# Part of the first shift by matrix products at step 1, and products of ones at the start, in a two-layer encoder kernel on one core

## The chip, the cores and the metric

The kernel runs on one core of a Trainium2 chip. The metric is the device time of one execution in microseconds (us); lower is better. The engines are TensorE (PE; its weight loads are shown as PEld), VectorE (DVE), ScalarE (ACT), GpSimd (POOL) and SyncE (SP), which issues the DMAs. Each engine runs its own list of instructions, and semaphores order the lists against each other.

## The reference, cut to what matters

Two layers of a streaming encoder, 256 tokens by 1024 channels. The part that matters here is the head of layer 0: a vector c is turned into six vectors by a matrix product, and the first two of them scale and shift the normalised input before the input projection.

```python
c_act = jax.nn.silu(c)
mod = jnp.dot(c_act, w_mod[layer]) + b_mod[layer]
sh1, sc1, g1, sh2, sc2, g2 = jnp.split(mod[:, None, :], 6, axis=-1)
u = rms_norm(x, norm1_g[layer]) * (1.0 + sc1) + sh1
x = x + g1 * token_mixers(u, ...)      # projection by w_in, three mixers, merge
u = rms_norm(x, norm2_g[layer]) * (1.0 + sc2) + sh2
x = x + g2 * grouped_moe(u, ...)       # 16 experts, 2 per token
```

Everything is float32; `w_mod` is 1024 x 6144, so `sh1` and `sc1` each need 4 MB of weights before the last channel of `u` is known.

## The kernel before, in words

The program is one list of calls per engine; the order in the code is the order on each engine (the schedule is manual). Weights come as blocks of up to 1 MB in the order of `plan`, through seven buffers `raw0` to `raw6`; SP issues the next block when a buffer has been given back, so a block lands some way ahead of its use.

Layer 0 begins with `prologue`: loads, constants, the row `crow` (c spread to 128 partitions by PE, L355, and put through SiLU by ACT, L357), then the sums of squares of x (ACT squares, L480, and PE products with a single column, L489). `rstd` (L524, L526) and `spread` (L534, L536) make of them the factor that every channel is multiplied by.

The first shift and scale are computed in two ways. `mod_rows` (L453) does it by DVE: 256 rows of the transposed weights against `crow`, two dot products over 1024 numbers, then the bias (L463) and for the scale one more instruction (L466). `mod_matmul` (L426) does it by PE: two blocks of 512 columns, eight products, then a copy by ACT (`mod_copy`, L433), four transposes by PE, a sum by DVE and the bias (`mod_finish`, L440, L442, L463). In the kernel before, all of the first shift and scale comes from `mod_rows`; later vectors of both layers use `mod_matmul`.

The start of the projection is cut into four steps (in `mixers`, layer 0). Step s takes two of the eight groups of 128 channels. It calls `mod_rows(0, s)` for the shift and `mod_rows(0, 4 + s)` for the scale, then one part of `modulate`: `uv` by DVE (L566), its high part `uh` by ACT (L567), its low part `ul` by DVE (L570). Then for each of three column blocks, gB0, gB1 and bi, `split_to` cuts half a weight block into a high part `h` by ACT (a CAST, L282) and a low part by DVE (a subtraction, L283), and PE makes the products (gB0 and gB1: 24 each, L615, L617, L618; bi: 12, L596 to L598). Nothing is split ahead in these steps. After step 1 `rotary` makes cosines and sines (L413 to L416). After step 3 the blocks' results are copied out by ACT (L924), and the next blocks (bq and on) follow, with a `mod_matmul` after bi.

`heat(n)` (L1180) issues n products of the identity by itself, whose result is not used; the kernel before calls it in the routing part of each layer and at the end of layer 0.

Of the kernel before, what the change touches and what calls it, by code (L numbers as in the profile page):

```python
# [10 lines left out]
F32 = mybir.dt.float32  # L11
# [97 lines left out]
WARM_IN = 1  # L109
HEAT_END = 4  # L110
HEAT_AFTER = 8


INNER = 'FVTS'
# [54 lines left out]
class Kernel:  # L169
# [30 lines left out]
    def t(self, pool, shape, dt, tag, bufs=1):  # L200
        return pool.tile(shape, dt, tag=tag, name=self.nm(tag), bufs=bufs)
# [101 lines left out]
    def prologue(self):  # L303
        nc, g, a = self.nc, self.g, self.a
        t = self.t
        self.sm = t(g, [128, SM_W], F32, "sm")
        nc.sync.dma_start(self.sm, a["smalls"])
        self.S = {k: self.sm[:, o:e] for k, (o, e) in SM.items()}
        self.cact_row()
        self.posi = t(g, [128, 2], I32, "posi")  # L310
        nc.sync.dma_start(self.posi, a["positions"])
        self.xT = t(g, [128, KT, T], F32, "xT")
        nc.sync.dma_start(self.xT, a["x"])
        self.pump()
        self.junk = t(g, [128, 1], F32, "junk")
        self.eps = t(g, [128, 1], F32, "eps")
        nc.vector.memset(self.eps, EPS)
        self.table(AF.Silu)
        self.ident = t(g, [128, 128], F32, "ident")
        make_identity(nc, self.ident)  # L320
        self.fold = t(g, [128, 16], F32, "fold")
        nc.vector.tensor_reduce(self.fold, self.ident.rearrange("p (q r) -> p r q", q=4)[:, 0:16], axis=AX.X, op=ALU.add)
        self.ones = t(g, [128, 128], F32, "ones")
        nc.vector.memset(self.ones, 1.0)
        self.ones_bf = t(g, [128, 128], BF16, "onesbf")
        nc.vector.memset(self.ones_bf, 1.0)
        self.tri = t(g, [128, 128], BF16, "tri")
        nc.vector.memset(self.tri, 1.0)
        nc.gpsimd.affine_select(self.tri, self.tri, pattern=[[1, 128]], compare_op=ALU.is_gt,
                                fill=0.0, base=0, channel_multiplier=-1)  # L330
        self.slot = t(g, [128, 128], F32, "slot")
        nc.gpsimd.iota(self.slot, pattern=[[1, 128]], base=-1024, channel_multiplier=0,
                       allow_small_or_imprecise_dtypes=True)
        self.up16 = t(g, [128, 16], F32, "up16")
        nc.gpsimd.iota(self.up16, pattern=[[1, 16]], base=0, channel_multiplier=0,
                       allow_small_or_imprecise_dtypes=True)
        self.down16 = t(g, [128, 16], F32, "down16")
        nc.gpsimd.iota(self.down16, pattern=[[-1, 16]], base=15, channel_multiplier=0,
                       allow_small_or_imprecise_dtypes=True)
        self.part = t(g, [128, 1], F32, "part")  # L340
        nc.gpsimd.iota(self.part, pattern=[[0, 1]], base=0, channel_multiplier=1, allow_small_or_imprecise_dtypes=True)
        self.mod = [t(g, [128, 6, 8], F32, f"mod{l}") for l in range(L)]
        self.scale = [[t(g, [128, 8], F32, f"sc{l}{j}") for j in range(2)] for l in range(L)]
# [89 lines left out]
        self.nc.scalar.copy(sb, acc)  # L433
        return sb

    def mod_finish(self, l, c, sb):
        nc = self.nc
        tp = self.psum("t")
        for b in range(4):
            nc.tensor.transpose(tp[:, 128 * b:128 * b + 128], sb[:, 128 * b:128 * b + 128], self.ident)  # L440
        j, k0 = divmod(4 * c, 8)
        nc.vector.tensor_reduce(self.mod[l][:, j, k0:k0 + 4],  # L442
                                tp.rearrange("p (b q r) -> p b q r", b=4, q=4)[:, :, :, 0], axis=AX.X, op=ALU.add)
        self.mod_bias(l, j, k0, 4)
# [438 lines left out]
    def mixers(self, l, parts, angles):  # L883
        nc, a = self.nc, self.a
# [3 lines left out]
        t = self.t  # L888
# [139 lines left out]
        if l == 0:  # L1028

            tags = iter(("mm", "mm", "mm", "y", "y", "y"))  # L1030
            for s in range(4):
                if s:
                    self.mod_rows(0, s)
                    self.mod_rows(0, 4 + s)
                next(parts)
                if s == 3:
                    self.ahead = AHEAD
                for i, c in enumerate(ORDER[:N_SPLIT]):
                    if s == 0:
                        open_chunk(c, tags, fine=True)  # L1040
                    next(gens[c])
                    if s == 3:
                        step_done(N_SPLIT + i, c, 1)
                if s == 1:
                    self.rotary(*angles)
            order = order[2 * N_SPLIT:]
        else:
            self.ahead = 0
            for s in range(4):
                next(parts)  # L1050
                if s == 3:
                    self.ahead = AHEAD
                for i, c in enumerate(ORDER[:N_EDGE]):
                    if s == 0:
                        open_chunk(c, iter(("mm", "mm") if i == 0 else ("mm", "y") if i == 1 else ("y", "y")), fine=True)
                    next(gens[c])
                    if s == 3:
                        step_done(N_EDGE + i, c, 1)
            order = order[2 * N_EDGE:]
# [113 lines left out]
        for c in "ckptmu":  # L1173
            assert next(acts[c], None) is None, c

    def heat(self, n):

        ps = self.hot if self.hot is not None else self.psum("mm")
        for _ in range(n):
            self.nc.tensor.matmul(ps[:, :128], self.ident, self.ident, start=True, stop=True)  # L1180

    def choose(self, l, aff, sel):

# [440 lines left out]
    def plan(self):  # L1624
# [27 lines left out]
        for l in range(L):  # L1652
            order = list(enumerate(half_order(l)))
            first = len(self.stream)
            if l == 0:
                for s in range(4):
                    rows(0, s).halved = 2
                    rows(0, 4 + s).halved = 2
                    for i, c in enumerate(ORDER[:N_SPLIT]):
                        n = COLS[c][1]  # L1660
                        key = ("in", l, c, s // 2)
                        if s % 2 == 0:
                            u = Unit(key, block("w_in", l, c, s // 2, n), n)
                            u.halved = 1
                            self.stream.append(u)
                        else:
                            u = Unit(("rest", *key), None)
                            u.rest = next(x for x in self.stream if x.key == key)
                            self.stream.append(u)
                            u = u.rest  # L1670
                        self.preps.append((u, s % 2))
                        if s == 3:
                            fill(0, N_SPLIT + i)
                order = order[2 * N_SPLIT:]
            together = []
            for s, (c, h) in order:
# [45 lines left out]
    def build(self):  # L1722
# [3 lines left out]
        for l in range(L):  # L1726
            with tc.tile_pool(name=f"w{l}", bufs=1) as self.w:
                if l == 0:
                    self.prologue()
                    self.fill_columns()  # L1730
                    self.fill_row()
                    angles = self.angles()
                    self.lam = self.lambdas()
                    next(self.lam)
                    acc = self.psum("y")
                    for k in range(4):
                        self.sum_squares(acc, k)
                    self.mod_rows(0, 0)
                    for k in range(4, KT):
                        self.sum_squares(acc, k)  # L1740
                    self.table(AF.Sqrt)
                    self.mod_rows(0, 4, (0,))
                    self.mod_rows(0, 4, (1,))
                    rstd = self.spread(self.rstd(acc), "t")
                rt = self.mixers(l, self.modulate(rstd, self.scale[l][0], self.mod[l][:, 0]), angles)
            with tc.tile_pool(name=f"e{l}", bufs=1) as self.e:
                self.slots += self.parts
                self.once += ONCES
                self.ye, self.ye_turn = None, 0
                self.parts = []  # L1750
                self.pump()
                self.where = {}
                self.route(l, rt)
                self.experts(l)
                self.parts = [x for x in self.slots if x[0] == "h"] + self.parts
                self.slots = [x for x in self.slots if x[0] == "r"]
            self.e = None
            rst = self.rstd(self.acc)
            if l == 0:
                self.heat(HEAT_END)  # L1760
            rstd = self.spread(rst, "y")
            if l == 0:
                self.heat(HEAT_AFTER)
# [64 lines left out]
```

## Time and profile before

| | us |
|---|---|
| median of 3 runs | 1067.27 (1066.63 to 1067.83) |
| profiled execution | 1067.82 |
| its span, first to last instruction | 1066.0 |
| PE busy | 1018.6 (96%) |
| DVE busy | 598.0 (56%) |
| ACT busy | 388.8 (36%) |
| DMA queue of loads, share of 16 engines | 79.8% |

A row of the time line gives the start, the time covered, the engine, the line, the operation, output<-input, and xN for N instructions merged; brackets give the idle time before it and what ended that. A row of the table of stretches gives the busy time of each engine in a stretch with its number of instructions, then TensorE's granted clock (1.00 is the higher of its two levels, 0.50 the lower, and between them a mean of both), the busy share of the DMA engines, and GB/s. A float32 product shows as two MATMUL rows.

### The profile page before, as it was taken

How to read it: one execution, taken by the hardware profiler on the slowest of the kernel's cores; microseconds unless marked ns; L12 is line 12 of the kernel's file. 1: busy time of each engine (PE TensorE's matmuls, PEld its weight loads, DVE VectorE, ACT ScalarE, POOL GpSimd, SP SyncE). 2: the span in 40 equal slices, each digit the busy share in tenths (PEclk: the TensorE clock that was granted, in tenths of full speed). 3: DMA queues.
4: the chain of work that ended last, by engine and by line, in shares of the span. 5: the costliest groups of instructions: out<-in, count | busy, mean ns of one | idle time of the engine just before them, and what ended most of it. 6: DMA issues, size and time to landing. Idle time of an engine off the chain costs nothing. (4 is left out here: it accounts for less than half of the span.)

```text
span 1066.0 us, 18867 instructions
## 1 busy us (share of the span) xinstructions
PE 1018.6 (96%) x7550; PEld 703.6 (66%) x7550; DVE 598.0 (56%) x1414; ACT 388.8 (36%) x736; POOL 1.5 (0%) x11
## 2 busy tenths in 40 slices
PE   7899999999999999799999999999998999979996
PEld 5789778799974343343489887789997534324344
DVE  6968898678842232222255799986885313222224
ACT  4445566654531111010245456675453201001022
POOL 0000000000000000000000000000000000000000
PEclk9999999999999999999989999999999999999998
DMA  9986768787967999999946465567784799999981
GB/s 345 366 353 236 269 263 336 297 335 277 353 245 306 395 420 421 420 420 421 403 176 242 194 237 198 198 224 279 307 339 163 304 397 420 420 419 420 422 351 40
DMA packets 53845, 336.56 MB, mean 316 GB/s; under 512 B 5617, under 2 KB 11889, under 8 KB 15474
## 3 DMA queue, kind: packets, MB, share of 16 engines
q1 hardware_dynamic: 53746, 335.25, 79.8%
q8 instruction: 61, 1.00, 0.4%
q14 instruction: 38, 0.31, 0.1%
HBM read 334.18 MB, written 1.05 MB: 314 GB/s over the span
## 5 line engine op out<-in xcount | busy, mean ns | idle before, releaser
L283 DVE TENSOR_TENSOR h<-raw,h 128x1024 fp32r<-128x1024 f32 (+1 forms) x132 | 154.7, 1213 | 32.0 <-ACT h L282 31.9
L1455 PE MATMUL mm<-raw,gb 128*32 128x512 f32 (+1 forms) x640 | 160.9, 596 | 1.6 <-DMA raw<-in_exp_w_dram 1.6
L615 PE MATMUL mm<-uh,h 128*128 128x256 f32 x480 | 138.9, 289 | 5.8 <-ACT h L282 5.8
L618 PE MATMUL mm<-uh,h 128*128 128x256 f32 x480 | 137.3, 286 | 2.7 <-DVE h L283 2.7
L282 ACT CAST h<-raw 128x1024 fp32r<-128x1024 f32 (+1 forms) x132 | 131.0, 1041 | 20.2 <-PE mm L618 9.8
L617 PE MATMUL mm<-ul,h 128*128 128x256 f32 x480 | 136.6, 285 | 0.0
L1535 DVE TENSOR_TENSOR x<-y,x 128x512 fp32r<-128x512 f32 (+1 forms) x34 | 22.5, 660 | 158.5 <-ACT x L1534 158.5
L1455 PE MATMUL mm<-h,gb 128*32 128x512 f32 (+1 forms) x376 | 101.4, 595 | 0.0
L615 PEld LDWEIGHTS mm<-uh,h 128*128 128x128 f32 x480 | 92.1, 192 | 11.8 <-ACT h L282 7.5
L1421 DVE SCALAR_TENSOR_TENSOR xT<-y,mod,xT 128x256 f32<-128x256 f32 x128 | 53.2, 477 | 73.7 <-PE y L1546 73.7
L1455 PE MATMUL mm<-x,gb 128*32 128x512 f32 (+1 forms) x456 | 94.5, 595 | 0.0
L618 PEld LDWEIGHTS mm<-uh,h 128*128 128x128 f32 x480 | 91.9, 192 | 3.7 <-DVE h L283 3.6
L617 PEld LDWEIGHTS mm<-ul,h 128*128 128x128 f32 x480 | 92.1, 192 | 0.0
L1455 PE MATMUL y<-raw,gt 128*32 128x512 f32 (+2 forms) x424 | 89.4, 570 | 1.4 <-ACT gt L1429 1.4
L1455 PEld LDWEIGHTS mm<-raw,gb 128*32 128x32 f32 (+1 forms) x640 | 41.1, 116 | 56.1 <-issue 49.9
L596 PE MATMUL mm<-h,uh 128*128 128x512 f32 (+1 forms) x176 | 70.7, 402 | 0.0
L597 PE MATMUL mm<-h,uh 128*128 128x512 f32 (+1 forms) x176 | 69.1, 393 | 0.0
L598 PE MATMUL mm<-h,ul 128*128 128x512 f32 (+1 forms) x176 | 69.1, 393 | 0.0
L1455 PE MATMUL y<-x,gt 128*32 128x512 f32 (+2 forms) x232 | 64.7, 580 | 0.7 <-ACT gt L1429 0.7
L453 DVE SCALAR_TENSOR_TENSOR raw<-raw,crow 128x1024 f32<-128x1024 f32 x52 | 62.0, 1219 | 1.0 <-ACT uv L480 1.0
L1365 ACT ACTIVATE gb<-y,mod,sc 128x256 f32<-128x256 f32 (+1 forms) x40 | 20.9, 521 | 107.5 <-DVE gb L1367 107.5
L1429 ACT COPY gt<-t 128x512 f32<-128x512 f32 x16 | 9.4, 585 | 128.1 <-PE t L1428 128.1
(317 smaller groups left out, 2008.2 us busy)
## 6 DMA issues: line engine op xcount, KB each, us to landing
raw<-in_exp_w_dram SPq DMA_DIRECT2D x77, 1024.0 KB, 15.5
x<-in_exp_w_dram SPq DMA_DIRECT2D x48, 1024.0 KB, 15.4
raw<-in_w_in_dram SPq DMA_DIRECT2D x43, 1024.0 KB, 5.1
h<-in_exp_w_dram SPq DMA_DIRECT2D x39, 1024.0 KB, 18.2
raw<-in_w_mod_dram SPq DMA_DIRECT2D x19, 1024.0 KB, 6.0
raw<-in_w_modt_dram SPq DMA_DIRECT2D x18, 1024.0 KB, 4.9
uh<-in_exp_w_dram SPq DMA_DIRECT2D x12, 1024.0 KB, 15.8
ul<-in_exp_w_dram SPq DMA_DIRECT2D x10, 1024.0 KB, 19.7
```

Of the source, the lines that this page charges most:

```text
L282: nc.scalar.copy(hi[:, :, :u.n], src)
L283: nc.vector.tensor_sub(lo[:, :, :u.n], src, hi[:, :, :u.n].bitcast(F32))
L453: nc.vector.scalar_tensor_tensor(v[:, b], v[:, b], 1.0, self.crow, op0=ALU.mult, op1=ALU.mult, accum_out=self.mod[l][:, j, k0 + b:k0 + b + 1])
L596: nc.tensor.matmul(o, uh, hi[:, k, :u.n], start=(kk == 0), stop=False)
L597: nc.tensor.matmul(o, uh, lo[:, k, :u.n], start=False, stop=False)
L598: nc.tensor.matmul(o, ul, hi[:, k, :u.n], start=False, stop=(kk == 7))
L615: nc.tensor.matmul(o, hi[:, k, cs], mh[kk], start=(kk == 0 and b % 2 == 0), stop=False, skip_group_check=True)
L617: nc.tensor.matmul(o, hi[:, k, cs], ml[kk], start=False, stop=False, skip_group_check=True)
L618: nc.tensor.matmul(o, lo[:, k, cs], mh[kk], start=False, stop=(kk == 7), skip_group_check=True)
L1421: nc.vector.scalar_tensor_tensor(self.xT[:, k + b], ps[:, T * b:T * b + T], self.mod[l][:, 5, k + b:k + b + 1], self.xT[:, k + b], op0=ALU ...
L1455: self.nc.tensor.matmul(o[c:c + step], lhs[:, c:c + step], x, start=start, stop=stop, skip_group_check=True)
L1535: self.nc.vector.tensor_sub(yl, ps, yh.bitcast(F32))
```

## The change

Four calls of `heat` are added at the start of layer 0: six products of a matrix of ones as soon as that matrix is set (its memset becomes DVE's first instruction), two products of the identity after the product in `lambdas`, six after `rstd` has been issued and before the product of `spread`, eight after that product. All write one PSUM tile that nobody reads.

At step 2 and step 3 `mod_rows(0, 2)` and `mod_rows(0, 3)` are gone. In their place `mod_matmul(0, 1)` computes those 512 numbers of the shift at step 1, on PE behind the products of gB1; ACT's copy follows in ACT's list, and `mod_finish` comes after the products of bi. The two blocks of `w_mod` stand in the stream after step 1's blocks, and the two blocks of transposed weights that fed steps 2 and 3 are gone; the bytes are the same.

```diff
+HEAT_START = (6, 2, 6, 8)
...
         self.pump()
+        self.ones = t(g, [128, 128], F32, "ones")
+        nc.vector.memset(self.ones, 1.0)
+        self.hot = self.psum("mm")
+        self.heat(HEAT_START[0], self.ones)
...
             for s in range(4):
+                if s == 1:
+                    self.mod_rows(0, s)
                 if s:
-                    self.mod_rows(0, s)
                     self.mod_rows(0, 4 + s)
                 next(parts)
...
                     if s == 3:
                         step_done(N_SPLIT + i, c, 1)
+                    if s == 1 and i == 1:
+                        first = self.mod_matmul(0, 1, "t")
+                        held["mod"] = self.mod_copy(first)
                 if s == 1:
+                    self.mod_finish(0, 1, held.pop("mod"), first)
                     self.rotary(*angles)
...
                 for s in range(4):
-                    rows(0, s).halved = 2
+                    if s < 2:
+                        rows(0, s).halved = 2
                     rows(0, 4 + s).halved = 2
...
+                    if s == 1:
+                        mod(0, 1)
                 order = order[2 * N_SPLIT:]
...
                     next(self.lam)
+                    self.heat(HEAT_START[1])
                     acc = self.psum("y")
...
-                    rstd = self.spread(self.rstd(acc), "t")
+                    rst = self.rstd(acc)
+                    self.heat(HEAT_START[2])
+                    rstd = self.spread(rst, "t")
+                    self.heat(HEAT_START[3])
+                    self.hot = None
```

On ACT at step 1 the kernel before has the three casts of gB0, gB1 and bi (weights `raw_83`, `raw_85`, `raw_87`) next to each other, then the table load and the sines:

```order
L567 ACTIVATE uh_214<-uv_313,mod_124 128x256
L282 CAST h_318<-raw_83 128x1024
L282 CAST h_347<-raw_85 128x1024
L282 CAST h_377<-raw_87 128x2x452
L413 ACT_TABLE_LOAD
```

The changed kernel has at the same place, with its own numbers and line numbers:

```order
L571 ACTIVATE uh_235<-uv_335,mod_131 128x256
L284 CAST h_340<-raw_83 128x1024
L284 CAST h_369<-raw_85 128x1024
L437 COPY modsb_415<-t_398 128x512
L284 CAST h_417<-raw_87 128x2x452
L417 ACT_TABLE_LOAD
```

The copy of the new product's result stands ahead of the cast of bi; what it copies is written by the eight products, which stand on PE between the last product of gB1 and the first of bi.

On DVE, from step 1's subtraction for bi to step 2's first `uv`, the kernel before has (`raw_177` feeds the shift, `raw_200` the scale):

```order
L283 TENSOR_TENSOR h_377<-raw_87,h_377 128x2x452
L415 COPY cos_398<-cos_398 128x2x32
L416 TENSOR_SCALAR sin_399<-sin_399 128x2x32
L453 SCALAR_TENSOR_TENSOR raw_177,mod_124<-raw_177,crow_71 128x1024 x2
L463 TENSOR_TENSOR mod_124<-mod_124,sm_69 128x2
L453 SCALAR_TENSOR_TENSOR raw_200,mod_124<-raw_200,crow_71 128x1024 x2
L463 TENSOR_TENSOR mod_124<-mod_124,sm_69 128x2
L466 SCALAR_TENSOR_TENSOR sc_126<-mod_124,sm_69 128x2
L566 SCALAR_TENSOR_TENSOR uv_415<-xT_75,sc_126,t_211 128x256
```

The changed kernel, at the same place:

```order
L285 TENSOR_TENSOR h_417<-raw_87,h_417 128x2x452
L446 TENSOR_REDUCE mod_131<-t_398 128x4
L467 TENSOR_TENSOR mod_131<-mod_131,sm_69 128x4
L419 COPY cos_440<-cos_440 128x2x32
L420 TENSOR_SCALAR sin_441<-sin_441 128x2x32
L457 SCALAR_TENSOR_TENSOR raw_322,mod_131<-raw_322,crow_71 128x1024 x2
L467 TENSOR_TENSOR mod_131<-mod_131,sm_69 128x2
L470 SCALAR_TENSOR_TENSOR sc_133<-mod_131,sm_69 128x2
L570 SCALAR_TENSOR_TENSOR uv_452<-xT_75,sc_133,t_224 128x256
```

The pair of dot products for the shift and its bias are gone, and the sum over the transposed product, with a bias of its own, comes ahead of the cosines and the remaining pair.

## Rows read from the trace of the kernel before

**Rows 1.** Table of stretches; columns as told above.
```profile
core 0: us, PE busy (x) PEld busy (x) DVE busy (x) ACT busy (x) POOL busy (x), PEclk, DMA share, GB/s
...
30.00:40.00 10.00, 9.25 (x64) 8.27 (x62) 9.41 (x19) 4.04 (x6) 0.00 (x0) 1.00 0.92 317
...
56.00:60.00 4.00, 4.00 (x25) 4.00 (x25) 0.23 (x1) 0.95 (x3) 0.00 (x0) 0.66 0.90 344
...
60.00:160.00 100.00, 100.00 (x664) 78.54 (x662) 85.51 (x235) 54.00 (x109) 0.00 (x0) 1.00 0.72 276
```

**Rows 2.** Time line of DVE, steps 1 to 3 and after.
```profile
30.60 3.37 DVE L283 TENSOR_TENSOR h<-raw,h 128x1024 fp32r<-128x1024 f32 x3 [0.45 <-ACT h L282]
...
34.22 1.22 DVE L453 SCALAR_TENSOR_TENSOR raw<-raw,crow 128x1024 f32<-128x1024 f32 x1
...
36.70 1.22 DVE L453 SCALAR_TENSOR_TENSOR raw<-raw,crow 128x1024 f32<-128x1024 f32 x1
...
41.89 3.37 DVE L283 TENSOR_TENSOR h<-raw,h 128x1024 fp32r<-128x1024 f32 x3 [0.45 <-ACT h L282]
...
52.86 3.37 DVE L283 TENSOR_TENSOR h<-raw,h 128x1024 fp32r<-128x1024 f32 x3 [0.45 <-ACT h L282]
62.99 2.36 DVE L283 TENSOR_TENSOR h<-raw,h 128x1024 fp32r<-128x1024 f32 x2 [6.76 <-ACT h L282]
...
73.08 0.17 DVE L442 TENSOR_REDUCE mod<-t 128x4 f32<-128x16 f32 x1
```

**Rows 3.** Time line of ACT after step 3.
```profile
61.42 0.59 ACT L924 COPY sg<-y 128x512 f32<-128x512 f32 x1 [0.84 <-PE y L618]
61.91 2.00 ACT L282 CAST h<-raw 128x1024 fp32r<-128x1024 f32 x2
...
69.23 0.59 ACT L433 COPY modsb<-mm 128x512 f32<-128x512 f32 x1
```

**Rows 4.** DMA issues from 20.5 to 22 us: size, us from issue to landing.
```profile
raw<-in_w_modt_dram SPq DMA_DIRECT2D x1, 512.0 KB, 11.3
```

**Rows 5.** Time line of SP in the same stretch.
```profile
20.66 0.33 SPq L243 DMA_DIRECT2D raw<-in_w_modt_dram  x1
```

**Rows 6.** Time line of PE, steps 1 to 3 and after.
```profile
37.45 0.37 PE L596 MATMUL y<-h,uh 128*128 128x452 f32 x1
...
39.72 0.37 PE L598 MATMUL y<-h,ul 128*128 128x452 f32 x1
...
43.17 0.39 PE L618 MATMUL mm<-uh,h 128*128 128x256 f32 x1 [0.76 <-DVE h L283]
...
51.00 0.37 PE L598 MATMUL y<-h,ul 128*128 128x452 f32 x1
...
54.14 0.39 PE L618 MATMUL mm<-uh,h 128*128 128x256 f32 x1 [0.75 <-DVE h L283]
...
63.49 0.37 PE L598 MATMUL y<-h,ul 128*128 128x452 f32 x1
63.79 1.92 PE L426 MATMUL mm<-raw,cact 128*32 128x512 f32 x16
...
71.34 0.60 PE L440 MATMUL t<-ident,modsb 128*128 128x128 f32 x4
```

**Rows 7.** Time line of PE at the start, and four products of `heat` later.
```profile
3.11 3.75 PE L355 MATMUL t<-crow,ones 1*128 1x512 f32 x4 [3.11 <-DMA crow<-in_crow_dram]
...
7.84 6.99 PE L489 MATMUL y<-ones,uv 128*128 128x1 f32 x32 [0.24 <-ACT uv L480]
15.98 1.22 PE L536 MATMUL t<-uv,ones 128*128 128x256 f32 x2 [1.14 <-DVE uv L534]
...
548.89 2.05 PE L1180 MATMUL mm<-ident 128*128 128x128 f32 x8
```

**Rows 8.** Time line of DVE at the start.
```profile
13.95 0.16 DVE L466 SCALAR_TENSOR_TENSOR sc<-mod,sm 128x2 f32<-128x2 f32 x1
15.16 0.17 DVE L526 RECIPROCAL rst<-rst 128x2 f32<-128x2 f32 x1 [1.05 <-ACT rst L524]
```

More of the change, by code (lines that the diff above doesn't have):

```diff
@@ L322, in prologue @@
         nc.vector.tensor_reduce(self.fold, self.ident.rearrange("p (q r) -> p r q", q=4)[:, 0:16], axis=AX.X, op=ALU.add)
-        self.ones = t(g, [128, 128], F32, "ones")
-        nc.vector.memset(self.ones, 1.0)
         self.ones_bf = t(g, [128, 128], BF16, "onesbf")
@@ L434, in mod_copy, with mod_finish @@
         return sb
-    def mod_finish(self, l, c, sb):
+    def mod_finish(self, l, c, sb, tp=None):
         nc = self.nc
-        tp = self.psum("t")
+        tp = self.psum("t") if tp is None else tp
         for b in range(4):
@@ L1174, in route, with heat @@
             assert next(acts[c], None) is None, c
-    def heat(self, n):
+    def heat(self, n, x=None):
         ps = self.hot if self.hot is not None else self.psum("mm")
         for _ in range(n):
-            self.nc.tensor.matmul(ps[:, :128], self.ident, self.ident, start=True, stop=True)
+            self.nc.tensor.matmul(ps[:, :128], self.ident if x is None else x, self.ident if x is None else x, start=True,
+                                  stop=True)
     def choose(self, l, aff, sel):
```

## The prediction, made before the changed kernel ran

> **What bounds the kernel now.** I read the table of stretches first. From 30 to 40 us DVE is busy for 9.41 of 10 us, and from 60 to 160 us PE is never idle while the DMA engines are busy for 0.72 of the time [rows 1]. So DVE sets the pace of the four opening steps, PE that of the stage behind them, and a delay at the end of step 3 reaches PE's list with nothing to swallow it. The time line of DVE gives the steps: step 1 starts its three subtractions at 30.60 and ends them at 33.97, step 2 starts at 41.89, step 3 at 52.86 [rows 2]. Between them stand the dot products: the pair for a shift takes from 34.22 to 36.70, 2.48 us, and the pair for a scale with one part of `modulate` from 36.70 to 41.89, 5.19 us [rows 2]. PE's time line shows the other side: PE finishes gB1 of step 1 only at 37.45 [rows 6], when DVE has been past step 1's subtractions for 3.5 us and is at work on step 2's dot products. That lead of DVE over PE is what the change touches.
>
> **The DVE work that goes.** Two pairs at 2.48 us, 4.96 us in all, one at step 2 and one at step 3. What comes back on DVE is one sum over 128x16 numbers, 0.17 us [rows 2], and a bias of about 0.16 us (taken from L466, a like instruction, [rows 8]): 0.33 us. Were this all, step 3 would start 4.6 us sooner.
>
> **The wait that comes.** The eight products stand on PE behind gB1, ACT's copy waits for them, and behind the copy in ACT's list stands the cast of bi. Behind that cast on DVE stand the subtraction for bi, the sum, the cosines and every dot product that is left. So DVE's lead is lost: it must stop after gB1's subtraction and wait until PE has caught up. Step by step, on the clock of the trace of before:
> - PE is through with gB1 at 37.45 [rows 6]. Eight products: 1.92 us, the row of sixteen MATMUL rows at 63.79 [rows 6], to 39.37. Copy 0.59 us [rows 3], to 39.96. Cast of bi 1.00 us (two in 2.00, [rows 3]), to 40.96. DVE's subtraction, a third of 3.37 us [rows 2], to 42.08. Before, it ended at 33.97. DVE has stood still from 32.85 to 40.96, 8.1 us.
> - Of bi's twelve products eleven need the low part, at a spacing of 0.206 us (39.72 less 37.45 over 11, [rows 6]): the last starts at 44.14 and takes 0.37 us, to 44.51. Four transposes, 0.60 us [rows 6], to 45.11. Sum and bias, to 45.44. Cosines and sines take 0.25 us as before (33.97 to 34.22), to 45.69. The pair for the scale and `modulate`, 5.19 us: step 2's subtractions start at 50.88, against 41.89.
> - Step 2 to step 3 took 10.97 us on DVE and takes 2.48 us less now, 8.49: step 3 starts at 59.37, against 52.86, so 6.5 us late.
>
> DVE thus gives back 2.48 us twice and loses about 11.5. The two new blocks are not the cause: they stand where the transposed blocks for step 2 stood, the last of which was issued at 20.66 and landed 11.3 us later, at 31.96 [rows 4, 5], 5.5 us before PE comes to them. Later blocks come into buffers that PE or DVE give back before the step that uses them is reached, and the engines are later now; I put them at nothing, and a cast that waits for a DMA would show otherwise.
>
> The Trainium skill says of the same thing (TensorE: Matmul & The Clock Gate, section "Architectural detail: the array is 16× 32×32, not 1× 128×128") that ScalarE and VectorE take their queues strictly in order and that only PE draws weight loads forward; this rule speaks against the change. The trace agrees: after step 3 DVE stands idle for 6.76 us for a cast [rows 2] that begins at 61.91, the moment the copy from PE's result at 61.42 lets ACT go on [rows 3]. By the rule the step-3 loss is the 6.5 us above; without it the sum would be that of the first rival.
>
> **What PE makes of it.** The first product that needs a low part starts 1.28 us after the subtractions (43.17 less 41.89), and the step's last one 7.83 us after that (51.00 less 43.17) [rows 2, 6]. Step 3 of before took 9.35 us for the same (63.49 less 54.14): 1.52 us more, in a stretch whose granted clock is 0.66, a mean of the higher level and the lower one, after PE had been nearly idle between step 2 and step 3 [rows 1, 6]. In the changed kernel PE is idle from 45.11 to 52.16 but for two products, longer than that, so I charge step 2 the same 1.52 us: its last product starts at 52.16 + 7.83 + 1.52 = 61.51. DVE would let step 3 go at 59.37 + 1.28 = 60.65, so PE itself is now later; with no idle time ahead step 3 runs at the higher clock, and with its two early products (0.12 us each: 7.83 less 11 times 0.206, over 46) and one spacing of 0.21 its last product starts at 69.8, against 63.49: 6.3 us late. With no charge DVE decides, and it is 68.48, 5.0 us late; with a charge of twice 1.52, 7.8 us late.
>
> **The products of ones and of the identity.** They can help in one place: the chain from sums of squares to `spread`. The sums take 6.99 us from 7.84 and the reciprocal comes at 15.16 [rows 7, 8]. But DVE is at its own dot products until 14.11 (13.95 and 0.16), so at most 1.05 us is to be had there, and 0.6 if the 1.22 us of `spread`'s product halve: 1.65 us gained at best. They cost if the clock stays low. Four such products took 2.05 us in the slowest row [rows 7], 0.51 each. Six from about 1.2 us (an estimate: PE has nothing before 3.11) end at 4.3, so `crow`'s product is 1.2 late; two more delay the sums by 1.0; six behind the sums cost 3.07, less the 1.15 us between the sums' end at 14.83 and 15.98. Together 4.1 us lost at worst. The eight after `spread` lie where PE waits for the first cast. The sums, one column at a time, ran low through their 6.99 us after the 3.75 us of `crow`'s product, so I don't expect the whole gain. I take 0.5 us lost, nearer the middle than either end, as rows bear out neither. A faster PE in step 0 gives nothing, since DVE is the later engine there.
>
> On this term the Trainium skill (same page, section "What's actually happening") says that the moment at which the clock rises shifts from run to run, since it isn't tied to the kernel's start. By it the start term would differ between executions; no run here shows it, as there is one trace.
>
> **Sum.** 6.3 + 0.5 = 6.8 us later at the end of step 3, and PE-bound from there. The profiled execution took 1067.82 us (span 1066.0 and 1.8 around it); that gives 1074.6. The median of the runs is 0.55 us below the profiled one: 1074.1 us.
>
> **Rivals.**
> - The cast of bi isn't held up, or the wait for PE costs less than DVE saves. Then step 3 starts 4.6 us sooner on DVE; PE, with 2.52 us more in step 1 (1.92 and 0.60), ends that step at 42.6 and, without its idle times, step 3 at about 59.0 against 63.9: about 4.8 us faster, 1062.5. For it: DVE is the busy engine, and its dot products do leave. Against: the order on ACT, and the 6.76 us of a like wait. It decides if the cast starts before 33.
> - The delay is swallowed: if some later stage is paced by loads that don't depend on this one, 0 to 1 us slower, 1067.8. For it: the DMA engines run at 0.92 here in places [rows 1]. Against: 0.72 from 60 to 160 us means that loads wait for buffers, and buffers come free later too.
> - The clock is worse than I charge: the start term at 4.1 and step 2 at twice 1.52 give 11.9 us, 1079.2.
>
> **Chances.** Forecast 0.75, its own range 1070.6 (5.0 less 1.65) to 1078; first rival 0.08; second 0.07; third 0.10. The range of 1070.0 to 1078.5 leaves out the first two and half of the third. A difference of 0.2%, about 2.1 us, is what a measurement of this kernel tells from no change: faster 0.08, within it 0.06, slower 0.86.
>
> **What would show it.** Right: on ACT a cast of bi at step 1 that starts about 0.6 us after the eight products end; on DVE an idle gap of 7 to 9 us ahead of step 1's last subtraction; step 2's subtractions near 51 and step 3's near 59; PE's last product of step 3 near 70; from there the same lengths as before. The start term is read from `spread`'s product (15.98 if nothing moves it). Wrong: a DVE gap under 3 us, step 3 before 53, or a shift at 70 us that is gone by the end.

## The result, and the profile after

| | before | after |
|---|---|---|
| median of the four runs, us | 1066.95 (1066.36 to 1067.83) | 1076.86 (1074.11 to 1077.65) |
| profiled execution, us | 1067.82 | 1077.65 |
| its span, us | 1066.0 | 1075.6 |

The changed kernel is slower, 1.0088 times the time of before, with a 95% interval of 1.0068 to 1.0107. That is 9.9 us between the medians; the forecast was 6.8, and 1076.86 lies inside its own range of 1070.6 to 1078.

The wait is found first. The page's group of the subtractions on DVE has gone from 32.0 us of idle time ahead of them to this:

```profile
L285 DVE TENSOR_TENSOR h<-raw,h 128x1024 fp32r<-128x1024 f32 (+1 forms) x132 | 154.8, 1212 | 38.7 <-ACT h L284 37.1
```

The time line of DVE (columns as in [rows 2], which it answers) shows where the idle time lies:

```profile
16.42 0.17 DVE L530 RECIPROCAL rst<-rst 128x2 f32<-128x2 f32 x1 [2.27 <-ACT rst L528]
...
19.75 0.87 DVE L570 SCALAR_TENSOR_TENSOR uv<-xT,sc,t 128x256 f32<-128x256 f32 x2 [2.57 <-PE t L540]
...
33.10 2.36 DVE L285 TENSOR_TENSOR h<-raw,h 128x1024 fp32r<-128x1024 f32 x2 [0.45 <-ACT h L284]
43.49 1.10 DVE L285 TENSOR_TENSOR h<-raw,h 128x904 fp32r<-128x904 f32 x1 [8.03 <-ACT h L284]
47.65 0.17 DVE L446 TENSOR_REDUCE mod<-t 128x4 f32<-128x16 f32 x1 [3.06 <-PE t L444]
...
53.33 3.37 DVE L285 TENSOR_TENSOR h<-raw,h 128x1024 fp32r<-128x1024 f32 x3 [0.45 <-ACT h L284]
...
61.82 3.37 DVE L285 TENSOR_TENSOR h<-raw,h 128x1024 fp32r<-128x1024 f32 x3 [0.45 <-ACT h L284]
```

Two of step 1's three subtractions go as before. Then DVE stands for 8.03 us ahead of bi's, does 1.10 us of work, and stands for 3.06 us more ahead of the sum. Step 1 began 2.50 us late (33.10 against 30.60), step 2 11.44 us late, step 3 8.96 us late.

The time line of ACT (same columns; it answers [rows 3]) names the cause:

```profile
42.03 0.58 ACT L437 COPY modsb<-t 128x512 f32<-128x512 f32 x1 [8.01 <-PE t L430]
42.51 0.95 ACT L284 CAST h<-raw 128x904 fp32r<-128x904 f32 x1
```

The bracket at DVE's gap says that it waits for ACT, but ACT is not busy: it stands 8.01 us itself, with the copy at the head of its list, until PE has made the eight products. The cast that DVE wants is one place behind the copy.

The time line of PE, which answers [rows 7] and [rows 6]:

```profile
1.25 2.93 PE L1189 MATMUL mm<-ones 128*128 128x128 f32 x12 [1.25 <-DVE eps L323]
4.11 3.78 PE L359 MATMUL t<-crow,ones 1*128 1x512 f32 x4
...
9.26 6.83 PE L493 MATMUL y<-ones,uv 128*128 128x1 f32 x32
15.95 2.91 PE L1189 MATMUL mm<-ident 128*128 128x128 f32 x12
18.65 1.06 PE L540 MATMUL t<-uv,ones 128*128 128x256 f32 x2
...
34.38 0.39 PE L622 MATMUL mm<-uh,h 128*128 128x256 f32 x1 [0.76 <-DVE h L285]
...
40.04 1.92 PE L430 MATMUL t<-raw,cact 128*32 128x512 f32 x16
43.51 0.47 PE L600 MATMUL y<-h,uh 128*128 128x452 f32 x1 [1.55 <-ACT h L284]
...
47.02 0.60 PE L444 MATMUL t<-ident,modsb 128*128 128x128 f32 x4
...
53.35 0.58 PE L619 MATMUL mm<-uh,h 128*128 128x256 f32 x1 [5.74 <-ACT h L284]
...
54.61 0.58 PE L622 MATMUL mm<-uh,h 128*128 128x256 f32 x1 [0.47 <-DVE h L285]
...
63.61 0.36 PE L602 MATMUL y<-h,ul 128*128 128x452 f32 x1
...
72.08 1.92 PE L430 MATMUL mm<-raw,cact 128*32 128x512 f32 x16
```

PE comes to the eight products at 40.04 with no bracket, so neither a DMA nor another engine held it there. After the transposes it has nothing for 5.74 us. The `mod_matmul` behind step 3 begins at 72.08, against 63.79 in [rows 6]: 8.29 us late. I use this product as the mark of what the opening costs. The table of stretches shows what the idle time brings:

```profile
48.00:52.00 4.00, 0.00 (x0) 0.00 (x0) 3.71 (x12) 0.54 (x2) 0.00 (x0) 0.79 1.05 422
52.00:56.00 4.00, 2.18 (x8) 1.89 (x9) 3.55 (x5) 3.09 (x4) 0.00 (x0) 0.50 1.02 430
56.00:60.00 4.00, 4.00 (x31) 4.00 (x30) 3.89 (x9) 0.07 (x1) 0.00 (x0) 0.86 0.25 102
```

After a stretch with no product at all the granted clock is 0.50, the lower level. Step 2's products go at it until about 57, and from the first product with a low part to the last they take 9.00 us (54.61 to 63.61), against 7.83.

From there the delay is carried as it is, 8.0 to 8.5 us as far as the start of layer 1. Some of the rest comes in layer 1, where PE waits for the blocks of the experts' weights. The row gives the total, the number of waits and the longest:

```profile
PE mm L1465 <- DMA raw<-in_exp_w_dram: 4.1, 2, 3.3
```

Before, the two waits at this line came to 1.6 us. So 2.5 us of this execution are a later wait for loads.

### The profile page after: what moved, and what is told of

Same layout as the page of the kernel before. It is cut to its first block, busy times and chain, and to the rows that moved or that the text cites. A ratio compares the mean times of both kernels' runs of the same rounds, so it can differ in the third digit from the quotient of the medians.

```text
span 1075.6 us, 18986 instructions
## 1 busy us (share of the span) xinstructions
PE 1025.6 (95%) x7614; PEld 709.9 (66%) x7614; DVE 593.2 (55%) x1406; ACT 389.4 (36%) x737; POOL 1.5 (0%) x11
## 5 line engine op out<-in xcount | busy, mean ns | idle before, releaser
L457 DVE SCALAR_TENSOR_TENSOR raw<-raw,crow 128x1024 f32<-128x1024 f32 x48 | 57.2, 1218 | 0.2 <-ACT uv L484 0.2
```

The lines of the kernel that those rows point to most:

```text
L457: nc.vector.scalar_tensor_tensor(v[:, b], v[:, b], 1.0, self.crow, op0=ALU.mult, op1=ALU.mult, accum_out=self.mod[l][:, j, k0 + b:k0 + b + 1])
```

## The experiments

My theory: the change costs by the order of ACT's list (DVE loses its lead and has to wait for PE), then by the lower clock that follows PE's idle time, and a little by the products of `heat`. Rivals: the products of `heat` are the main cost; the eight products themselves are too much for PE; or the dot products that leave DVE save nothing. None of the kernels leaves any part of the computation out. The kernel before, run beside them, took 1066.66 us (median of 17 runs) with the first four and 1066.42 (17) with the last four. The two sets ran on different chips, so a run of one set is compared with a run of the other by what each is above the kernel before beside it.

| run | median, us | ratio to before, 95% |
|---|---|---|
| e1_no_heat | 1075.81 | 1.0081 (1.0068 to 1.0094) |
| e2_heat_only | 1069.58 | 1.0027 (1.0015 to 1.0040) |
| e3_cast_first | 1070.51 | 1.0029 (1.0017 to 1.0041) |
| e4_no_wait | 1061.78 | 0.9955 (0.9939 to 0.9971) |
| e5_hot_wait | 1073.27 | 1.0064 (1.0049 to 1.0079) |
| e6_hot_wait_heat | 1074.30 | 1.0081 (1.0060 to 1.0101) |
| e7_last_heat | 1067.56 | 1.0008 (0.9998 to 1.0019) |
| e8_after | 1076.78 | 1.0096 (1.0079 to 1.0112) |

**e1_no_heat**: the changed kernel without the four calls.

```diff
-HEAT_START = (6, 2, 6, 8)
+HEAT_START = (0, 0, 0, 0)
```

> The changed kernel with all four added calls of heat set to none; the matrix products for the shift at step 1 stay. My theory (the added products delay the sums of squares and spread's product by 2.7 us, and the wait at step 1 costs the rest): spread's product is back near 16.0, DVE's idle gap ahead of step 1's last subtraction stays at 8.0 us, step 2's subtractions start near 50.8 and step 3's near 59.3, and the median is about 2.5 us under the changed kernel's, some 1074.4 (7.4 over the kernel before). Rival A (the added products pay for themselves by raising the clock of step 0): without them the median is no lower than 1076.9. Rival B (the added products are the whole loss): the median falls to 1067.

Most of the loss stays: 8.6 us by the ratio, 9.15 between the medians. So the products of `heat` are not the main cost, and less goes away with them than the 2.5 us I expected. Its table of stretches says why:

```profile
44.00:48.00 4.00, 1.31 (x9) 0.96 (x7) 2.62 (x7) 0.00 (x0) 0.00 (x0) 0.91 1.04 398
48.00:52.00 4.00, 0.79 (x2) 0.50 (x2) 3.26 (x9) 2.84 (x5) 0.00 (x0) 0.50 1.02 430
52.00:56.00 4.00, 3.69 (x17) 3.69 (x18) 4.00 (x6) 0.80 (x1) 0.00 (x0) 0.50 0.71 295
```

DVE's steps are 2.3 us earlier than in the changed kernel (step 2 at 51.03, with the same gap of 8.02), but step 2's first product with a low part now starts at 52.31 and the products keep their longer times until about 57.4: some 5 us at the lower level, against some 2.4 in the changed kernel. The mark shows a gain of only 1.14 us:

```profile
70.94 1.92 PE L430 MATMUL mm<-raw,cact 128*32 128x512 f32 x16
```

**e2_heat_only**: the kernel before with the four calls and nothing else of the change.

```diff
+HEAT_START = (6, 2, 6, 8)
...
+                    self.heat(HEAT_START[1])
...
+                    rst = self.rstd(acc)
+                    self.heat(HEAT_START[2])
+                    rstd = self.spread(rst, "t")
+                    self.heat(HEAT_START[3])
```

> The kernel before with the four added calls of heat alone; the shift is all by DVE's dot products as before. My theory: spread's product starts near 18.6 against 15.98, everything behind it keeps its distances, median 1069.5 (2.5 over the kernel before). Rival A: the clock is up through step 0 and 1 and gives it back, 1067. Rival B (they add nothing by themselves and only shift the moments at which the clock falls): within 1 us of 1067, either side.

The median is 2.9 us above before, as expected. In its trace DVE's first `uv` stands where it stands in the changed kernel, 2.5 us later than before:

```profile
19.74 0.87 DVE L570 SCALAR_TENSOR_TENSOR uv<-xT,sc,t 128x256 f32<-128x256 f32 x2 [2.57 <-PE t L540]
```

The mark of this execution is only 0.99 us late, though, as the stretch of lower clock fell elsewhere. It is also the fastest of the eleven (1067.14 us), so the trace does not show where the 2.9 us of the median come from. The clock was at 0.66 from 56 to 60 in [rows 1]; here it is at 1.00 there, and low from 32 to 40, under products of step 1, for which DVE does not wait in this order:

```profile
64.78 1.92 PE L430 MATMUL mm<-raw,cact 128*32 128x512 f32 x16
```

```profile
32.00:36.00 4.00, 2.12 (x9) 1.92 (x10) 3.55 (x5) 3.98 (x5) 0.00 (x0) 0.80 0.35 110
```

**e3_cast_first**: no `heat`, and the cast and subtraction of bi are issued ahead of the eight products and the copy.

```diff
                     if s == 1 and i == 1:
+                        self.warm(1)
                         first = self.mod_matmul(0, 1, "t")
```

> Without the added calls of heat, as in the first of these four; in addition the cast and the subtraction of bi's half block are issued ahead of the copy at step 1, so that the copy holds no cast back. My theory (what DVE waits for is PE catching up; the cast is only the first thing in its way, the sum over the transposed product is the next): the 8 us gap ahead of the subtraction goes, a gap of about 8.5 us opens ahead of the sum, because the transposes still stand behind bi's products; only PE's own pause for bi goes, so step 2's subtractions start near 48.1 against 50.8, and the median is 2.7 us under the first of these four, about 1071.7. Rival (the cast behind the copy is the whole cause): DVE keeps its lead, step 2 starts near 42 and the median is under 1067.

The 8 us ahead of bi's subtraction are gone, since all three subtractions run together. The next instruction that needs PE takes the wait over, the sum:

```profile
30.61 3.37 DVE L285 TENSOR_TENSOR h<-raw,h 128x1024 fp32r<-128x1024 f32 x3 [0.45 <-ACT h L284]
42.68 0.17 DVE L446 TENSOR_REDUCE mod<-t 128x4 f32<-128x16 f32 x1 [8.70 <-PE t L444]
```

Step 2 starts at 48.36 (48.1 expected), and the median is 5.3 us below e1 and still 3.9 above before. I had expected 2.7 below e1; the traces show 3.0 of the 5.3 at the mark (67.93 against 70.94), and the rest is not explained. The order on ACT is a cause, but only the first of two; whoever mends it alone finds the second.

**e4_no_wait**: no `heat`; nothing of DVE waits for PE any more. The weights of step 1 are cast and subtracted first (`warm(3)`), the eight products and their copy stand ahead of gB0 on PE, the transposes behind gB0, and the sum only at step 2, behind the dot products for the scale. The cosines follow at the end of step 2.

```diff
+                if s == 2:
+                    self.mod_sum(0, 1, first)
                 next(parts)
...
+                if s == 1:
+                    self.warm(3)
+                    first = self.mod_matmul(0, 1, "t")
+                    held["mod"] = self.mod_copy(first)
...
-                    if s == 1 and i == 1:
-                        first = self.mod_matmul(0, 1, "t")
-                        held["mod"] = self.mod_copy(first)
-                if s == 1:
-                    self.mod_finish(0, 1, held.pop("mod"), first)
+                    if s == 1 and i == 0:
+                        self.mod_turn(held.pop("mod"), first)
+                if s == 2:
                     self.rotary(*angles)
```

> Without the added calls of heat; at step 1 the casts and subtractions of all three half blocks are issued first, the eight products stand on PE ahead of gB0 (in the time in which it waits for the subtraction anyway), the transposes behind gB0, the sum on DVE behind step 2's dot products for the scale, and the sines go to the end of step 2. My theory (the saving on DVE is real once DVE never waits for PE): no DVE gap over 1 us between 30 and 45 us, step 2's subtractions near 39.5 against 41.9, PE without idle time from 31 to 58, step 3's last product near 58 against 63.5, median about 1061.5, 5.5 us faster than the kernel before. Rival A (the blocks for the new products land too late, near 32, and PE and then step 2 slip): 1064 to 1067. Rival B (loads of the following blocks can't come sooner and the gain is lost there): 1067.

It is 4.9 us faster than before and the fastest kernel of this study, 15 us below the changed kernel and 14 below e1, which has the same products on PE. DVE's time line has no bracket at the sum, and step 3 is 4.76 us earlier than in [rows 2]:

```profile
36.60 0.17 DVE L452 TENSOR_REDUCE mod<-t 128x4 f32<-128x16 f32 x1
...
39.27 3.37 DVE L285 TENSOR_TENSOR h<-raw,h 128x1024 fp32r<-128x1024 f32 x3 [0.45 <-ACT h L284]
...
48.10 3.37 DVE L285 TENSOR_TENSOR h<-raw,h 128x1024 fp32r<-128x1024 f32 x3 [0.45 <-ACT h L284]
```

PE pays 0.61 us for a block of `w_mod` that lands late, and has the mark 5.71 us earlier than before:

```profile
31.93 1.07 PE L430 MATMUL t<-raw,cact 128*32 128x512 f32 x8 [0.61 <-DMA raw<-in_w_mod_dram]
...
58.08 1.92 PE L430 MATMUL mm<-raw,cact 128*32 128x512 f32 x16
```

So the 4.6 us that the prediction put on DVE's dot products are real. They were there to be had, and the wait ate them. The 0.95 us beyond DVE's 4.76 come with the clock: no stretch from 40 to 68 is below 1.00, where before had 0.66 from 56 to 60. That returns the 1.52 us of step 3, less 0.57 because PE, now without idle time from step 2 to step 3, is the later engine (from 48.10 its last product of step 3 could start at 57.21, and by the mark it starts 0.57 later).

**e5_hot_wait**: e1 with twenty products of the identity in PE's idle time between the transposes and step 2.

```diff
                     self.mod_finish(0, 1, held.pop("mod"), first)
+                    self.hot = first
+                    self.heat(20)
+                    self.hot = None
```

> The changed kernel without its four added calls of heat, and with twenty products of the identity on PE behind the sum of step 1, in the time in which PE waits for step 2. My theory (in step 2 PE pays for the clock that falls while it waits): the granted clock stays at 1.00 from 44 to 64 us, step 2's last product comes 1.2 to 2.6 us sooner, DVE decides when step 3 starts (59.5), and the product that follows step 3 starts near 68.9 against 70.9; median some 2 us under the same kernel without the twenty, about 1073.8. Rival (the loss in step 2 is DVE's alone, or the twenty delay step 2): no change or slower, 1075.8 and more.

This measures the clock's part by itself: DVE's steps lie where e1 has them (step 2 at 51.09), PE is kept at work, and the granted clock stays at 1.00 from 40 to 64. The mark is 1.94 us earlier than in e1. The median is 6.85 us above before, against 9.15 in e1, but the intervals of the two ratios overlap, so it is the trace that carries this reading:

```profile
45.64 4.73 PE L1192 MATMUL t<-ident 128*128 128x128 f32 x40 [0.27 <-DVE mod L446]
...
69.00 1.92 PE L430 MATMUL mm<-raw,cact 128*32 128x512 f32 x16
```

```profile
48.00:52.00 4.00, 2.88 (x24) 2.48 (x22) 3.26 (x9) 2.78 (x5) 0.00 (x0) 1.00 1.01 424
52.00:56.00 4.00, 3.63 (x30) 3.63 (x31) 4.00 (x6) 0.86 (x2) 0.00 (x0) 1.00 0.70 287
```

**e6_hot_wait_heat**: the changed kernel with the same twenty products.

```diff
                     self.mod_finish(0, 1, held.pop("mod"), first)
+                    self.hot = first
+                    self.heat(20)
+                    self.hot = None
```

> The changed kernel with all its four calls of heat, and the same twenty products behind the sum of step 1. The start term measured 2.9 us by itself but only 1.05 on top of the matrix products for the shift. Theory A (the difference is a charge for the clock in step 2 that depends on the moment at which it rises again): with that charge gone in both, this kernel is 2.3 to 2.9 us over the one without the calls at the start, near 1076.3. Theory B (the calls at the start do something for the later steps that is worth 1.5 us): it is 1 us over, near 1074.9.

The median is 1.0 us above e5, with intervals that overlap, so the run doesn't tell the two theories apart. Its trace shows that the question was put wrongly. I had taken the start term for a constant of 2.5 us; here `crow`'s product took 2.10 us instead of 3.78 (the granted clock, 0.98 from 4 to 8, falls to 0.50 only behind it), and `uv` is only 0.76 us late:

```profile
4.11 2.10 PE L359 MATMUL t<-crow,ones 1*128 1x512 f32 x4
```

```profile
18.00 0.87 DVE L570 SCALAR_TENSOR_TENSOR uv<-xT,sc,t 128x256 f32<-128x256 f32 x2 [2.57 <-PE t L540]
```

```profile
69.48 1.92 PE L430 MATMUL mm<-raw,cact 128*32 128x512 f32 x16
```

**e7_last_heat**: the kernel before with the eight products after `spread` alone.

```diff
+HEAT_START = (0, 0, 0, 8)
```

> The kernel before with the last of the four added calls alone: eight products of the identity behind spread's product, where PE waits for the first cast. My theory (only those ahead of crow's product, the sums and spread cost): spread's product at 15.98, first uv at 17.24, the clock up before step 0's products, no time lost at the start and none gained, since DVE is the later engine in step 0: within 1 us of the kernel before, 1066.7. Rival (the eight hold up step 0's products): 1068 to 1069.

No difference that can be told from none. The eight products take 3.62 us in PE's idle time and push step 0's first product to 20.43, against 19.65 before; DVE is the later engine there and swallows it. The interval leaves the eight at most 2.0 us, so most of what `heat` costs by itself in e2 (2.9 us) lies in the other 14 products. The clock is low here from 44 to 48, under step 2, and the mark comes 1.38 us earlier than before:

```profile
16.15 1.22 PE L540 MATMUL t<-uv,ones 128*128 128x256 f32 x2 [1.14 <-DVE uv L538]
...
17.16 3.62 PE L1184 MATMUL mm<-ident 128*128 128x128 f32 x16
...
62.41 1.92 PE L430 MATMUL mm<-raw,cact 128*32 128x512 f32 x16
```

```profile
44.00:48.00 4.00, 4.00 (x24) 4.00 (x23) 3.97 (x8) 0.00 (x0) 0.00 (x0) 0.58 1.05 426
```

**e8_after**: the changed kernel as it is, for a second execution with a trace.

> The changed kernel unchanged, on the same chip as the three others, so that they can be compared with it: 1076.9 (1074 to 1077.7 so far), and its profile again. Where its trace shows step 2's first product with a low part at another place against the clock's fall and rise, the end of step 3 moves with it by up to 1.5 us; without that the end of step 3 is at 72.1 again.

The time is the same as in the first measurement, by another road. The clock was up when `crow`'s product came, so the reciprocal is 0.75 us earlier than in [rows 8] and `uv` only 0.50 late:

```profile
4.11 2.26 PE L359 MATMUL t<-crow,ones 1*128 1x512 f32 x4
```

```profile
14.41 0.17 DVE L530 RECIPROCAL rst<-rst 128x2 f32<-128x2 f32 x1 [0.27 <-ACT rst L528]
...
17.74 0.87 DVE L570 SCALAR_TENSOR_TENSOR uv<-xT,sc,t 128x256 f32<-128x256 f32 x2 [2.57 <-PE t L540]
...
42.83 1.10 DVE L285 TENSOR_TENSOR h<-raw,h 128x904 fp32r<-128x904 f32 x1 [9.39 <-ACT h L284]
```

Then step 1 ran in part at the lower level (0.57 from 32 to 36), and since DVE now waits for that step, its gap is 9.39 us. Step 2 was low as well, and the mark stands at 72.64, 8.85 us late:

```profile
72.64 1.92 PE L430 MATMUL mm<-raw,cact 128*32 128x512 f32 x16
```

## Why the prediction was right, and where its size was not

**The order on ACT, DVE's wait, steps 2 and 3: right.** The wait was put at 8.1 us and is 8.03. Without the 2.5 us of the start, step 2 is 8.94 us late (8.99 foretold) and step 3 6.46 (6.5). The cast of bi starts 0.55 us after the eight products end (40.04 and 1.92 give 41.96; the cast is at 42.51). e4 shows the other side: with the wait gone, the dot products that leave are worth what was said.

On the order, the Trainium skill (TensorE: Matmul & The Clock Gate, section "Architectural detail: the array is 16× 32×32, not 1× 128×128") says that ScalarE and VectorE take their queues strictly in order; the traces agree, with ACT's 8.01 us at the copy, and e3, where against e1 only the order was changed and the 8 us at the cast went.

**No cost by the new blocks, the eight products after `spread` at nothing, no gain from a faster step 0: right.** PE had no wait at 40.04; e7 shows the second; and step 1's subtractions begin 10.96 us after step 0's (22.14 to 33.10), with PE's products of step 0 spaced at 0.12 us, and 10.97 us in the trace of before (19.63 to 30.60), where most of them are spaced at 0.21.

**The end of step 3.** For five executions with the wait as the change makes it, the mark's delay comes apart as follows. The start is `uv`'s delay against 17.24, its place in the trace of before; step 1's clock is DVE's gap less 8.02; step 2's clock is what is left above 4.95, the value of e5, in which it is nothing, as it is in e6 (granted clock 1.00 from 40 to 64 in both). So 4.95 is measured in e5 and borrowed in after, e1 and e8; DVE's rows bear it out. In after, step 3's subtractions at 61.82 would let the mark come at 71.23 (1.28, 7.83 and 0.30 us later), and it comes at 72.08, 0.85 late.

| | start | step 1's clock | the wait itself | step 2's clock | the mark is late by |
|---|---|---|---|---|---|
| forecast | 0.5 | 0 | 5.0 | 1.3 | 6.8 |
| after | 2.51 | 0 | 4.95 | 0.83 | 8.29 |
| e1 | 0.20 | 0 | 4.95 | 2.00 | 7.15 |
| e5 | 0.26 | 0 | 4.95 | 0 | 5.21 |
| e6 | 0.76 | 0 | 4.93 | 0 | 5.69 |
| e8 | 0.50 | 1.37 | 4.95 | 2.03 | 8.85 |

The wait itself, against the one trace of before, was sized right to 0.05 us; the bound of 5.0 "with no charge" is what e5 and e6 measure. Three terms were not:

- The start term. "I take 0.5 us lost" was a choice between bounds of 1.65 gained and 4.1 lost. It was 2.51 in one execution and 0.50 in another of the same kernel (2.50 in e2 and 0.76 in e6, with the same four calls), so that 0.50 meets the forecast is luck. Read from the rows, the six products behind `rstd` cost 1.25 us in both (from the reciprocal to `uv` 3.33 us, before 2.08), where the forecast's worst case had 1.92. The first eight give between 0.75 gained and 1.26 lost, by whether the clock is up at 4.11. A certain loss of 1.25 should have been in the sum, and not only in the bound.
- The clock's charge. I charged one step, 1.52 us on PE and 1.3 net, by one row of before. It is 0.8 to 2.0 in step 2. What I had not thought of is that it strikes step 1 too (1.37 in e8): before, a longer step 1 is hidden, as DVE does not wait for PE there; in the changed kernel it is on the path. The forecast weighed the clock in PE's idle time alone.
- The trace to compare with. The 5.0 us count from a step 3 of before that itself lost 1.52 us to the clock. The two other traces with that order, e2 and e7, lost nothing there: less their late start, their marks stand at 62.28 and 62.24, not at 63.79. Against such an execution the wait itself costs 6.5 us, all that DVE loses. The forecast took one execution's loss for the rule.

On the start term the Trainium skill (same page, section "What's actually happening") says that the moment of the rise isn't tied to the kernel's start and shifts from run to run. Now there are traces for it, and they agree: the same product of the same kernel took 3.78 us in one execution and 2.26 in another.

**PE-bound from there: right for layer 0, not to the end.** In the first execution the delay is handed on whole until the experts of layer 1, where the wait for their loads grew from 1.6 to 4.1 us. It did not in e8 (1.4), so I don't count it as an effect of the change. In e8 the delay is 6.9 us early in layer 1 and 8.8 at the end, against the same trace of before.

**The rivals.** The gap of 8.03 us rules out the first, and a delay that lasts to the end rules out the second. Of the third, a worse clock, part came true: step 2's charge reached 2.0 us net (e1, e8), and the start term 2.5 of its 4.1.

**What stays open.** The traces of the changed kernel put the opening at 8.3 and 8.9 us, the medians the whole at 9.9 and 10.4. The remaining 1 to 2 us are not settled. Before has a single trace, at 1067.82, near the upper end of its runs (1063.92 to 1068.64 beside the experiments). If most of its executions lose nothing in step 3, as e2 and e7 did not, that would account for up to 1.5 us; the executions without a trace can't show it. Behind the mark the other executions differ from this trace by between 1.7 us less and 1.5 us more. What `heat` costs inside the changed kernel is not pinned down either: 2.9 us alone, but 0.8 to 1.2 by the medians (e1 against after and e8, e5 against e6, each by what it is above before), with intervals that overlap.

## What to carry to other kernels

Before work is moved from a busy engine to another, look for the first instruction in each list that will wait for the new result, and for everything behind it in that list: here 1.92 us of products on PE made DVE stand for 8 us, by a copy that stood one place ahead of a cast. DVE was the busier engine of these steps, yet moving work from it paid only where it didn't have to fetch the result before PE had caught up: with the products asked for early and their result fetched late (e4) the kernel is 4.9 us faster than before, and with the result fetched while PE is still behind (e1) 9.2 us slower. When one engine's lead over the other is lost, whatever it had hidden (a step at the lower clock among it) comes onto the path too, so the sum must be made anew for the steps that cost nothing before. And one trace of before is one execution: where the clock fell in it is not where it falls in the next.

## What was not expected of the hardware

- Products that keep PE busy from the first microsecond did not always raise the clock: in the first execution after, six products of ones took 2.93 us, `crow`'s then 3.78, and the sums, a column at a time, 6.83, all as slow as in [rows 7], while with the same instructions `crow`'s product took 2.10 and 2.26 us in e6 and e8.
- In e8 the clock was up for `crow`'s product and fell to its lower level under the sums of squares, with PE busy for 4.00 of 4 us:

```profile
8.00:12.00 4.00, 4.00 (x21) 4.00 (x21) 3.14 (x6) 2.81 (x7) 0.00 (x0) 0.52 1.02 404
12.00:16.00 4.00, 4.00 (x20) 4.00 (x20) 2.71 (x9) 0.94 (x3) 0.00 (x0) 0.50 1.01 355
```

- In the traces of before and of the first execution after, the granted clock stands at 1.00 from 0 to 16 us, although the products there take their longer times; at the very start the length of a product says more than the column.
- Twenty products of the identity, 4.73 us of work that nobody reads, gave back 1.94 us in the trace of e5 and cost nothing that it shows, since PE had been idle there. But e4, in which PE has no such idle time, is some 11.5 us faster than e5.
